# Attention scores of a two-layer decoder trunk: one fp32 product, or three products of high and low parts

## The chip, the cores and the metric

The kernel runs on one core of a Trainium2 chip. The core has five engines that run their own instruction streams and wait for each other by semaphores: TensorE (in the profile PE for the matmuls and PEld for the loads of the stationary operand), VectorE (DVE), ScalarE (ACT), GpSimd (POOL) and SyncE (SP, which here issues the large transfers). Data lies in an on-chip memory of 128 partitions; matmuls write into a second one, PSUM. The metric is the device time of one execution in microseconds, the median of several.

## The reference, cut to what matters

A batch of one sequence of 256 tokens of width 2048 goes through two layers: a Mamba-2 layer, and then a layer of sliding-window attention with 32 query heads of 64, 4 shared key/value heads and a sink per head. Each layer is added to its input, scaled, and normalized. The change touches the scores of the second layer only:

```python
proj = x @ w_in                                   # 2048 -> 2048 q, 2048 gate
q = _rope_partial(proj[..., :Q_WIDTH] + q_bias)    # 32 heads of 64
k, v = _shared_kv(x, kv_w, kv_b, cos, sin)         # 4 heads of 64
s = einsum("bcqhrd,bckhd->bchrqk", q, k) * 64 ** -0.5   # window 128, blocks of 128
s = where(valid, s, -inf)
m = maximum(max(s), sink);  p = exp(s - m)
p = p / (sum(p) + exp(sink - m))
o = (p @ v) * silu(gate)
return o @ w_out
```

## The kernel before, in words

All large matmuls work with split operands. A weight arrives in fp32 (`wr`), ScalarE rounds it to fp32r (`wh`, line 133), VectorE subtracts to get the rest (`wl`, line 134), and three products, high-high, high-low and low-high, are summed in PSUM (lines 195 to 197, 255 to 257, 704 to 706). fp32r is a rounded fp32 that TensorE multiplies in one pass; the profile prints it as f32. Weights come in units of 2048 columns, two units ahead of their use (`next_unit`), through 5 raw, 4 high and 4 low buffers. PSUM has four buffers `mm` for the large products and four buffers `ax` for everything else.

The first layer takes up to about 690 us. Then the normalized stream is held as x1H and x1L, and the second layer runs in blocks of four units, in the order of `B_ORDER`: queries of group j (`q_block`), gates of group j (`gate_block`), output projections ("o"). Group j is one key/value head with its 8 query heads. Smaller steps are put between the units by `later(n, fn)`: fn is called at the n-th `tick` from there, one tick per unit from the query blocks on. A scheduler then orders each engine's instructions and assigns the buffers: tiles of one tag share that tag's `bufs` buffers, and the next tile waits for all readers of the last.

The steps around the scores are these:
- The key/value projection writes `kd` (line 719) and `vt`; each key head is doubled so that it stands on partitions 0 to 63 and 64 to 127 after the transposes of `ktr` (line 731). ScalarE copies them from PSUM to `kT` (line 734).
- `q_block` adds the bias row (line 753, from a row that `bias_row` loads through POOL's queue, line 682), rotates, and one tick later `qtr` transposes (line 759) and ScalarE scales by 0.125 into `qT` (line 763). Two heads stand one above the other on the partitions.
- `attend(j, h)` follows for the half h of the sequence (128 rows): the score products with 64 rows (line 796), the halves of the partitions `par` 0 and 1, against 128 keys (h = 0) or 256 (h = 1); the mask addition from PSUM into `p` (line 801); the maximum (809), the exponentials on ScalarE (815), the division (820). `attend(j, 1)` comes three ticks after `attend(j, 0)`, for j = 3 one tick.
- Three ticks after attend, `turn_p` transposes p through PSUM (lines 829 to 836); later `pv` multiplies with the values (843) and the gate into `o` (849), which is split into oH and oL (858, 859) for the output projection.

The buffers that matter: `p0` and `p1` (one each, for h = 0 and 1), `qt` (two, for kd and the query tiles), `o` (one), `sg` (two, the gates), `bias` (two).

Of the kernel before, what the change touches and what calls it, by code (L numbers as in the profile page):

```python
# [8 lines left out]
F32 = mybir.dt.float32  # L9
F32R = mybir.dt.float32r  # L10
I32 = mybir.dt.int32
AF = mybir.ActivationFunctionType
ALU = mybir.AluOpType
AX = mybir.AxisListType

P = 128
S = 256
# [40 lines left out]
def trunk(ctx: ExitStack, tc: tile.TileContext, A: dict, out: bass.AP, dbg=None):  # L58
    nc = tc.nc
    PSUM = bass.MemoryType.PSUM  # L60

    def pool(name, bufs=1, side=None, space=None, stack=ctx):
        kw = {"space": space} if space is not None else {}
        return stack.enter_context(
            tc.tile_pool(name=name, bufs=bufs, side=side, reuse_waits="tile", **kw)
        )
# [9 lines left out]
    def nm(s):  # L76
        uid[0] += 1
        return f"{s}_{uid[0]}"

    def mm_tile():  # L80
        return mm_ps.tile([P, 512], F32, tag="mm", name=nm("mm"), bufs=4)
# [119 lines left out]
    def later(n, fn):  # L201
        pending.append([n, fn])
# [385 lines left out]
    for g in range(NG):  # L588
        t = 10 * g
# [86 lines left out]
    bp = pool("bp")  # L676
# [1 line left out]
    nc.gpsimd.dma_start(snk, A["snk"].partition_broadcast(P))  # L678

    def bias_row(src):  # L680
        t = bp.tile([P, 512], F32, tag="bias", name=nm("bias"), bufs=2)
        nc.gpsimd.dma_start(t[:], src.partition_broadcast(P))
        return t

# [14 lines left out]
    def x_stat(ps, h, u, ui):  # L699
        for k in range(4):  # L700
            kk = ui * 4 + k
            ks = slice(k * 512, (k + 1) * 512)
            hs = slice(h * P, (h + 1) * P)
            nc.tensor.matmul(ps[:], x1H[:, kk, hs], u.h[:, ks], start=kk == 0, stop=False)  # L704
            nc.tensor.matmul(ps[:], x1L[:, kk, hs], u.h[:, ks], start=False, stop=False)  # L705
            nc.tensor.matmul(ps[:], x1H[:, kk, hs], u.l[:, ks], start=False, stop=kk == KT - 1)  # L706


    kT = bp.tile([P, 4, S], F32, tag="kT", name="kT")
    vt = bp.tile([P, 2, S], F32, tag="vt", name="vt")  # L710
    kvb = bias_row(A["kvb"])
    kv_u = []
    for h in range(2):
        ps = mm_tile()
        for ui in range(4):
            if h == 0:
                kv_u.append(next_unit())
            x_stat(ps, h, kv_u[ui], ui)
        kd = bp.tile([P, 4, 2, 64], F32, tag="qt", name=nm("kd"), bufs=2)
        nc.vector.tensor_tensor(  # L720
            kd[:, :, 0, :], ps[:, :256].rearrange("p (j d) -> p j d", j=4),
            kvb[:, :256].rearrange("p (j d) -> p j d", j=4), ALU.add,
        )
        nc.vector.tensor_tensor(vt[:, h, :], ps[:, 256:], kvb[:, 256:], ALU.add)
        rope(kd[:, :, 0, :], h, 4)
        nc.gpsimd.tensor_copy(kd[:, :, 1, :], kd[:, :, 0, :])

        def ktr(h=h, kd=kd):
            pt = ax_tile()
            for j in range(4):  # L730
                nc.tensor.transpose(
                    pt[:, j * P : (j + 1) * P], kd[:, j, :, :].rearrange("p a d -> p (a d)"), ident
                )
            nc.scalar.copy(kT[:, :, h * P : (h + 1) * P], pt[:].rearrange("p (j t) -> p j t", j=4))

        later(2, ktr)

    qT = {}
    sg = {}
    os_ = {}  # L740

    def q_block(j):
        pss = [mm_tile(), mm_tile()]
        qb = bias_row(A["qb"][j * 512 : (j + 1) * 512])
        for ui in range(4):
            u = next_unit()
            for h in range(2):
                x_stat(pss[h], h, u, ui)
            tick()
        for h in range(2):  # L750
            qt = bp.tile([P, 8, 64], F32, tag="qt", name=nm("qt"), bufs=2)
            qf = qt[:].rearrange("p a d -> p (a d)")
            nc.vector.tensor_tensor(qf, pss[h][:], qb[:], ALU.add)
            rope(qt[:], h, 8)

            def qtr(h=h, qf=qf):
                pt = ax_tile()
                for p_ in range(4):
                    nc.tensor.transpose(
                        pt[:, p_ * P : (p_ + 1) * P], qf[:, p_ * P : (p_ + 1) * P], ident  # L760
                    )
                q2 = bp.tile([P, 4, P], F32, tag="qT", name=nm("qT"), bufs=2)
                nc.scalar.activation(
                    q2[:], pt[:].rearrange("p (a t) -> p a t", a=4), AF.Copy, scale=0.125
                )
                qT[j, h] = q2

            later(1, qtr)

# [14 lines left out]
    def attend(j, h):  # L784

        nk = P * (h + 1)
        q2 = qT[j, h]
        p = bp.tile([P, 8, nk], F32, tag=f"p{h}", name=nm("p"), bufs=1)
        mask = mask_a1 if h else mask_a0
        per = 512 // nk  # L790
        for b in range(0, 4, per):
            pss = [ax_tile(), ax_tile()]
            for i in range(per):
                for par in range(2):
                    rows = slice(64 * par, 64 * par + 64)
                    nc.tensor.matmul(
                        pss[par][:, i * nk : (i + 1) * nk], q2[rows, b + i, :], kT[rows, j, :nk],
                        start=True, stop=True,
                    )
            for par in range(2):  # L800
                nc.vector.tensor_tensor(
                    p[:, par * 4 + b : par * 4 + b + per, :],
                    pss[par][:].rearrange("p (a k) -> p a k", a=per),
                    mask.unsqueeze(1).to_broadcast([P, per, nk]), ALU.add,
                )
        sk = snk[:, j * 8 : j * 8 + 8]
        sm = bp.tile([P, 8, 8], F32, tag="sm", name=nm("sm"), bufs=2)
        mx, ng, rs, es, ri = [sm[:, i, :] for i in range(5)]
        nc.vector.tensor_reduce(mx, p[:], AX.X, ALU.max)
        nc.vector.tensor_tensor(mx, mx, sk, ALU.max)  # L810
        nc.vector.tensor_scalar(ng, mx, -1.0, None, ALU.mult)
        nc.vector.tensor_tensor(es, sk, ng, ALU.add)
        nc.scalar.activation(es, es, AF.Exp)
        for r in range(8):
            nc.scalar.activation(
                p[:, r, :], p[:, r, :], AF.Exp, bias=ng[:, r : r + 1], accum_out=rs[:, r : r + 1]
            )
        nc.vector.tensor_tensor(rs, rs, es, ALU.add)
        nc.vector.reciprocal(ri, rs)
        nc.vector.tensor_tensor(p[:], p[:], ri.unsqueeze(2).to_broadcast([P, 8, nk]), ALU.mult)  # L820

        pts = {}

        def turn_p():
            for kc in range(h + 1):
                for par in range(2):
                    pt = ax_tile()
                    for a in range(4):
                        nc.tensor.transpose(
                            pt[:, a * P : (a + 1) * P], p[:, par * 4 + a, kc * P : (kc + 1) * P], ident  # L830
                        )
                    t = bp.tile([P, 512], F32, tag="pt", name=nm("pt"), bufs=4)
                    if par:
                        nc.scalar.copy(t[:], pt[:])
                    else:
                        nc.vector.tensor_copy(t[:], pt[:])
                    pts[kc, par] = t

        def pv():
            ov = ax_tile()  # L840
            for kc in range(h + 1):
                for par in range(2):
                    nc.tensor.matmul(
                        ov[64 * par : 64 * par + 64, :], vt[:, kc, j * 64 : j * 64 + 64], pts[kc, par][:],
                        start=kc == 0, stop=kc == h,
                    )
            o = bp.tile([P, 4, P], F32, tag="o", name=nm("o"), bufs=1)
            hs = slice(h * P, (h + 1) * P)
            nc.vector.scalar_tensor_tensor(
                o[:], ov[:].rearrange("p (a t) -> p a t", a=4), 0.5, sg[j][:, :, hs], ALU.mult, ALU.mult  # L850
            )
            if j not in os_:
                os_[j] = (
                    bp.tile([P, 4, S], F32R, tag="oH", name=nm("oH"), bufs=2),
                    bp.tile([P, 4, S], F32R, tag="oL", name=nm("oL"), bufs=2),
                )
            oH, oL = os_[j]
            nc.scalar.activation(oH[:, :, hs], o[:], AF.Copy)
            nc.vector.tensor_tensor(oL[:, :, hs], o[:], oH[:, :, hs].bitcast(F32), ALU.subtract)

        last = j == 3
        later(3, turn_p)
        later(4 if last or h else 6, pv)
        if h == 0:
            later(1 if last else 3, lambda: attend(j, 1))
# [153 lines left out]
```

## Time and profile before

| what | value |
|---|---|
| median of the three runs | 1024.12 us |
| the three runs | 1023.79, 1024.12, 1253.01 us |
| the profiled execution's own time | 1023.71 us |
| its span, first to last instruction | 1021.9 us |
| mean granted TensorE clock | 0.997 of full speed |
| read from HBM | 200.13 MB, 198 GB/s over the span |
| score products (line 796): instructions, median duration | 128, 374 ns |
| score products: first and last start | 738.6 us, 954.7 us |

A row of the order of time has the start in us, the length in us, engine, line, operation, tiles (out<-in), rows*columns of the stationary operand, moving operand, and how many instructions are merged into the row; a bracket gives idle time before it and what ended it. A row of the groups has after the count the busy us and the mean ns of one, then the idle time before. A row of waits has the waiter, what it waited for, the total in us, how often, and the longest.

### The profile page before, as it was taken

The numbers are of one execution on the slowest core, as the hardware profiler recorded it, in microseconds if no ns is written. First come the engines' busy times: TensorE is split into PE (matmuls) and PEld (weight loads), VectorE is DVE, ScalarE is ACT, GpSimd is POOL, SyncE is SP. The second block draws the span as 40 slices with busy tenths as digits, with TensorE's granted clock in tenths as the row PEclk, the third lists the DMA queues.
The fourth block names the chain that finished last, engine by engine and source line by source line (L and its number), as shares of the span: only waits on it lengthen the run. The fifth ranks groups of instructions, "written<-read, shape, count | busy, mean of one in ns | idle before, by whom it ended". The sixth has DMA issues, their size and how long they took to land. (4 is left out here: it accounts for less than half of the span.)

```text
span 1021.9 us, 17613 instructions
## 1 busy us (share of the span) xinstructions
PE 1002.5 (98%) x7028; PEld 906.6 (89%) x7028; DVE 806.3 (79%) x1234; ACT 521.7 (51%) x795; POOL 84.9 (8%) x112
## 2 busy tenths in 40 slices
PE   7999999999999999999999999999999999999997
PEld 7998999999998998999999999878988878879975
DVE  6889897886895995986897797798577785785776
ACT  6565554744654554564464474535545453453642
POOL 0000303003003001100300300301000000000002
PEclk9999999999999999999999999999999999999999
DMA  8887585674764765666567466646555445545522
GB/s 307 281 301 241 167 270 176 226 235 141 260 212 143 266 202 192 213 208 219 178 207 239 159 196 229 241 145 234 195 167 170 154 142 182 173 142 182 193 97 82
DMA packets 55730, 203.50 MB, mean 199 GB/s; under 512 B 6288, under 2 KB 6560, under 8 KB 54880
## 3 DMA queue, kind: packets, MB, share of 16 engines
q1 hardware_dynamic: 54288, 196.33, 57.2%
q0 software_dynamic: 1072, 5.53, 1.6%
q8 instruction: 55, 0.90, 0.4%
q10 hardware_dynamic: 288, 0.52, 0.1%
q14 instruction: 27, 0.22, 0.1%
HBM read 200.13 MB, written 2.23 MB: 198 GB/s over the span
## 5 line engine op out<-in xcount | busy, mean ns | idle before, releaser
L134 DVE TENSOR_TENSOR wl<-wr,wh 128x1024 fp32r<-128x1024 f32 (+2 forms) x342 | 393.5, 1169 | 103.0 <-ACT wh L133 101.5
L133 ACT ACTIVATE wh<-wr 128x1024 fp32r<-128x1024 f32 (+2 forms) x342 | 338.0, 1012 | 230.8 <-PE mm L196 67.2
L195 PE MATMUL mm<-xH,wh 128*128 128x256 f32 x1296 | 361.7, 279 | 7.8 <-ACT wh L153 6.0
L197 PE MATMUL mm<-xH,wl 128*128 128x256 f32 x1296 | 360.3, 278 | 3.1 <-DVE wl L134 3.1
L196 PE MATMUL mm<-xL,wh 128*128 128x256 f32 x1296 | 360.7, 279 | 0.0
L195 PEld LDWEIGHTS mm<-xH,wh 128*128 128x128 f32 x1296 | 245.3, 189 | 9.8 <-ACT wh L153 6.3
L197 PEld LDWEIGHTS mm<-xH,wl 128*128 128x128 f32 x1296 | 245.2, 189 | 3.6 <-DVE wl L134 3.5
L196 PEld LDWEIGHTS mm<-xL,wh 128*128 128x128 f32 x1296 | 245.4, 189 | 1.1
L255 PE MATMUL mm<-wh,yH 128*128 128x512 f32 x256 | 101.4, 396 | 0.0
L256 PE MATMUL mm<-wh,yL 128*128 128x512 f32 x256 | 99.9, 390 | 0.0
L257 PE MATMUL mm<-wl,yH 128*128 128x512 f32 x256 | 99.7, 390 | 0.0
L482 POOL TENSOR_TENSOR yz<-yz,z 128x256 f32<-128x256 f32 x32 | 29.8, 931 | 538.5 <-DVE yz L475 538.5
L195 PE MATMUL mm<-x1H,wh 128*128 128x256 f32 x256 | 71.9, 281 | 0.0
L197 PE MATMUL mm<-x1H,wl 128*128 128x256 f32 x256 | 71.0, 277 | 0.0
L196 PE MATMUL mm<-x1L,wh 128*128 128x256 f32 x256 | 71.0, 277 | 0.0
L356 DVE SCALAR_TENSOR_TENSOR cv<-mm,pc,cv 128x255 f32<-128x255 f32 x144 | 68.6, 476 | 2.5 <-ACT cv L354 1.6
L704 PE MATMUL mm<-wh,x1H 128*128 128x512 f32 x160 | 63.3, 396 | 0.0
L706 PE MATMUL mm<-wl,x1H 128*128 128x512 f32 x160 | 62.7, 392 | 0.2 <-DVE wl L134 0.2
L705 PE MATMUL mm<-wh,x1L 128*128 128x512 f32 x160 | 62.7, 392 | 0.2 <-DVE x1L L668 0.2
L255 PEld LDWEIGHTS mm<-wh,yH 128*128 128x128 f32 x256 | 48.1, 188 | 10.3 <-DVE z L421 0.9
L257 PEld LDWEIGHTS mm<-wl,yH 128*128 128x128 f32 x256 | 48.1, 188 | 10.1
L256 PEld LDWEIGHTS mm<-wh,yL 128*128 128x128 f32 x256 | 48.1, 188 | 9.0
(181 smaller groups left out, 1308.5 us busy)
## 6 DMA issues: line engine op xcount, KB each, us to landing
wr<-in_wa SPq DMA_DIRECT2D x158, 512.0 KB, 5.2
wr<-in_wo SPq DMA_DIRECT2D x64, 512.0 KB, 5.3
rb<-rscr SPq DMA_DIRECT2D x32, 512.0 KB, 4.8
wr<-in_wq SPq DMA_DIRECT2D x32, 512.0 KB, 4.5
wr<-in_wg SPq DMA_DIRECT2D x32, 512.0 KB, 5.3
wr<-in_wb SPq DMA_DIRECT2D x32, 512.0 KB, 4.6
wr<-in_wkv SPq DMA_DIRECT2D x8, 512.0 KB, 6.6
first<-in_first SPq DMA_DIRECT2D x4, 512.0 KB, 8.8
```

What stands on the lines that cost most here:

```text
L133: nc.scalar.activation(h[:, sl], raw, AF.Copy)
L134: nc.vector.tensor_tensor(l[:, sl], raw, h[:, sl].bitcast(F32), ALU.subtract)
L195: nc.tensor.matmul(ps, ah, bh, start=first, stop=False)
L196: nc.tensor.matmul(ps, ah, bl, start=False, stop=False)
L197: nc.tensor.matmul(ps, al, bh, start=False, stop=last)
L255: nc.tensor.matmul(ps[:], aH[:, k, hs], u.h[:, ks], start=k == 0, stop=False)
L256: nc.tensor.matmul(ps[:], aL[:, k, hs], u.h[:, ks], start=False, stop=False)
L257: nc.tensor.matmul(ps[:], aH[:, k, hs], u.l[:, ks], start=False, stop=k == 3)
L356: nc.vector.scalar_tensor_tensor(a[:, sft:], ps[:, : S - sft], w(3 - sft), a[:, sft:], ALU.mult, ALU.add)
L704: nc.tensor.matmul(ps[:], x1H[:, kk, hs], u.h[:, ks], start=kk == 0, stop=False)
L705: nc.tensor.matmul(ps[:], x1L[:, kk, hs], u.h[:, ks], start=False, stop=False)
L706: nc.tensor.matmul(ps[:], x1H[:, kk, hs], u.l[:, ks], start=False, stop=kk == KT - 1)
```

## The change

Keys and queries are kept as a high part in fp32r and a low part, the rest in fp32r: `kH`, `kL` in place of `kT`, and `qH`, `qL` in place of `qT`. ScalarE writes the high part from PSUM, VectorE the low part from the same PSUM tile. The score product becomes a sum of three products with 64 rows: qH with kH, qL with kH, qH with kL, the two partition halves alternating. To make room, the bias rows have one buffer, both halves' `p` share one buffer of 8 x 256 (for j = 3, h = 0 `p` takes a buffer of the gates `sg`), and `o` uses the two `qt` buffers.

```diff
@@ -678,7 +678,7 @@
     nc.gpsimd.dma_start(snk, A["snk"].partition_broadcast(P))
 
     def bias_row(src):
-        t = bp.tile([P, 512], F32, tag="bias", name=nm("bias"), bufs=2)
+        t = bp.tile([P, 512], F32, tag="bias", name=nm("bias"), bufs=1)
         nc.gpsimd.dma_start(t[:], src.partition_broadcast(P))
         return t
 
@@ -706,7 +706,8 @@
             nc.tensor.matmul(ps[:], x1H[:, kk, hs], u.l[:, ks], start=False, stop=kk == KT - 1)
 
 
-    kT = bp.tile([P, 4, S], F32, tag="kT", name="kT")
+    kH = bp.tile([P, 4, S], F32R, tag="kH", name="kH")
+    kL = bp.tile([P, 4, S], F32R, tag="kL", name="kL")
     vt = bp.tile([P, 2, S], F32, tag="vt", name="vt")
     kvb = bias_row(A["kvb"])
     kv_u = []
@@ -731,7 +732,10 @@
                 nc.tensor.transpose(
                     pt[:, j * P : (j + 1) * P], kd[:, j, :, :].rearrange("p a d -> p (a d)"), ident
                 )
-            nc.scalar.copy(kT[:, :, h * P : (h + 1) * P], pt[:].rearrange("p (j t) -> p j t", j=4))
+            hs = slice(h * P, (h + 1) * P)
+            v = pt[:].rearrange("p (j t) -> p j t", j=4)
+            nc.scalar.activation(kH[:, :, hs], v, AF.Copy)
+            nc.vector.tensor_tensor(kL[:, :, hs], v, kH[:, :, hs].bitcast(F32), ALU.subtract)
 
         later(2, ktr)
 
@@ -759,11 +763,13 @@
                     nc.tensor.transpose(
                         pt[:, p_ * P : (p_ + 1) * P], qf[:, p_ * P : (p_ + 1) * P], ident
                     )
-                q2 = bp.tile([P, 4, P], F32, tag="qT", name=nm("qT"), bufs=2)
-                nc.scalar.activation(
-                    q2[:], pt[:].rearrange("p (a t) -> p a t", a=4), AF.Copy, scale=0.125
+                qH, qL = [bp.tile([P, 4, P], F32R, tag=t, name=nm(t), bufs=2) for t in ("qH", "qL")]
+                v = pt[:].rearrange("p (a t) -> p a t", a=4)
+                nc.scalar.activation(qH[:], v, AF.Copy, scale=0.125)
+                nc.vector.scalar_tensor_tensor(
+                    qL[:], v, 0.125, qH[:].bitcast(F32), ALU.mult, ALU.subtract
                 )
-                qT[j, h] = q2
+                qT[j, h] = qH, qL
 
             later(1, qtr)
 
@@ -784,19 +790,24 @@
     def attend(j, h):
 
         nk = P * (h + 1)
-        q2 = qT[j, h]
-        p = bp.tile([P, 8, nk], F32, tag=f"p{h}", name=nm("p"), bufs=1)
+        qH, qL = qT[j, h]
+        if j == 3 and h == 0:
+
+            p = bp.tile([P, 8, nk], F32, tag="sg", name=nm("p"), bufs=2)
+        else:
+            p = bp.tile([P, 8, S], F32, tag="p", name=nm("p"), bufs=1)[:, :, :nk]
         mask = mask_a1 if h else mask_a0
         per = 512 // nk
         for b in range(0, 4, per):
             pss = [ax_tile(), ax_tile()]
             for i in range(per):
-                for par in range(2):
-                    rows = slice(64 * par, 64 * par + 64)
-                    nc.tensor.matmul(
-                        pss[par][:, i * nk : (i + 1) * nk], q2[rows, b + i, :], kT[rows, j, :nk],
-                        start=True, stop=True,
-                    )
+                for n, (q2, k2) in enumerate(((qH, kH), (qL, kH), (qH, kL))):
+                    for par in range(2):
+                        rows = slice(64 * par, 64 * par + 64)
+                        nc.tensor.matmul(
+                            pss[par][:, i * nk : (i + 1) * nk], q2[rows, b + i, :], k2[rows, j, :nk],
+                            start=n == 0, stop=n == 2,
+                        )
             for par in range(2):
                 nc.vector.tensor_tensor(
                     p[:, par * 4 + b : par * 4 + b + per, :],
@@ -844,7 +855,7 @@
                         ov[64 * par : 64 * par + 64, :], vt[:, kc, j * 64 : j * 64 + 64], pts[kc, par][:],
                         start=kc == 0, stop=kc == h,
                     )
-            o = bp.tile([P, 4, P], F32, tag="o", name=nm("o"), bufs=1)
+            o = bp.tile([P, 4, P], F32, tag="qt", name=nm("o"), bufs=2)
             hs = slice(h * P, (h + 1) * P)
             nc.vector.scalar_tensor_tensor(
                 o[:], ov[:].rearrange("p (a t) -> p a t", a=4), 0.5, sg[j][:, :, hs], ALU.mult, ALU.mult
```

## The prediction

> **What bounds the kernel now.** I read the head of the page first, then the busy time by stretches over the attention part (from about 690 us), then who TensorE waited for there, and last the order of time around the scores.
>
> ```profile
> span 1021.9 us, 17613 instructions
> PE 1002.5 (98%) x7028; PEld 906.6 (89%) x7028; DVE 806.3 (79%) x1234; ACT 521.7 (51%) x795; POOL 84.9 (8%) x112
> ```
> ```profile
> 714.00:976.00 262.00, 260.89 (x1649) 223.40 (x1648) 186.03 (x291) 133.00 (x278) 2.14 (x4) 1.00 0.52 172
> ```
> ```profile
> PE ax L829 <- DVE o L849: 1.0, 1, 1.0
> PE mm L705 <- DVE x1L L668: 0.2, 1, 0.2
> ```
>
> The columns of the second fence are the stretch, its length, then busy us of PE, PEld, DVE, ACT and POOL, the granted clock and the DMA share. All score products lie in this stretch, PE has work in 260.9 of 262 us at full clock, and the third fence (waiter, releaser, us in total, times, longest) says that from 690 to 1010 us it waited 1.2 us in all. So a change here costs what it adds to PE's own instruction stream, plus any wait it creates. A matmul's duration is no price, since matmuls overlap; the price is the step from one start to the next.
>
> ```profile
> 740.51 0.28 PE L195 MATMUL mm<-x1H,wh 128*128 128x256 f32 x1
> ...
> 744.93 0.28 PE L195 MATMUL mm<-x1H,wh 128*128 128x256 f32 x1
> ```
> ```profile
> L195 PE MATMUL mm<-xH,wh 128*128 128x256 f32 x1296 | 361.7, 279 | 7.8 <-ACT wh L153 6.0 <-DVE cv L356 1.8
> L731 PE MATMUL ax<-cc,kd 128*128 128x128 f32 x8 | 1.0, 272 | 0.0
> ```
> ```profile
> 714.76 1.03 PE L731 MATMUL ax<-cc,kd 128*128 128x128 f32 x8
> ```
> ```profile
> 119.00 0.52 PEld L506 LDWEIGHTS ax<-cc,sq 128*128 128x128 f32 x4
> ```
>
> Between the two rows of the first fence lie 39 matmuls of 256 columns in the rounded fp32 type (fp32r, which the profile prints as f32): 4.42 / 39 = 0.113 us a step, in one pass. The weight load has a step of its own: four loads whose matmuls stream a single column each take (0.52 - 0.19) / 3 = 0.11 us, and eight transposes of 128 columns step at (1.03 - 0.27) / 7 = 0.109. So a matmul with few moving columns doesn't go below about 0.11 us here: I read this as the load binding it.
>
> **The scores as they are.** The order of time shows three of the eight bursts (PE, and PEld for the loads); a row merges what stands together, and its second column is the length.
>
> ```profile
> 738.61 1.16 PE L796 MATMUL ax<-kT,qT 64*128 64x128 f32 x16
> 739.70 0.39 PE L195 MATMUL mm<-x1H,wh 128*128 128x256 f32 x1
> ```
> ```profile
> 738.61 0.97 PEld L796 LDWEIGHTS ax<-kT,qT 64*128 64x128 f32 x16
> ```
> ```profile
> 953.11 2.00 PE L796 MATMUL ax<-kT,qT 64*128 64x256 f32 x16
> 955.03 0.39 PE L195 MATMUL mm<-x1H,wh 128*128 128x256 f32 x1
> ```
> ```profile
> 953.10 1.60 PEld L796 LDWEIGHTS ax<-kT,qT 64*128 64x128 f32 x16
> ```
> ```profile
> 757.17 1.16 PEld L796 LDWEIGHTS ax<-kT,qT 64*128 64x128 f32 x10 [0.17 <-PE ax L829]
> 758.83 0.73 PEld L796 LDWEIGHTS ax<-kT,qT 64*128 64x128 f32 x6 [0.51 <-ACT pt L834]
> 759.89 0.19 PEld L704 LDWEIGHTS mm<-wh,x1H 128*128 128x128 f32 x1 [0.33 <-issue]
> ```
> ```profile
> PEld ax L796 <- ACT pt L834: 1.3, 3, 0.5
> ```
>
> The code asks for 8 products per call of attend; the trace has 16. So an fp32 product is two instructions, and the two 64-row halves (`par`) go side by side: 16 instructions are 8 pairs. For the first half of the sequence (h = 0, 128 keys) the loads give (0.97 - 0.19) / 7 = 0.111 us a pair; for h = 1 (256 keys) the first step is a bare load of 0.11 and the rest (1.60 - 0.19 - 0.11) / 6 = 0.217. That is about twice the 256-column step of 0.113, so each instruction streams its columns twice, and one fp32 product streams them four times. A burst costs its pairs and about 0.20 us at its ends: 8 x 0.111 + 0.20 = 1.09 (739.70 - 738.61), 8 x 0.217 + 0.19 = 1.92 (955.03 - 953.11). For j = 0 to 2 (the last fence counts three) the h = 1 burst has a wait in its middle: the second group of two heads starts at 758.83, when ACT has emptied the transposes' buffer, and takes 1.06 us to 759.89.
>
> **The change part by part.**
>
> Scores, L796. Each product becomes three fp32r products of one pass, in the order high-high, low-high, high-low, halves alternating: 12 pairs for 8, and the loads grow from 8 to 12 with them. With 256 keys I take 0.113 a pair, the row of the same size and type. For j = 3: 12 x 0.113 - 8 x 0.217 = 1.36 - 1.74 = -0.38 us. For j = 0 to 2 the first group ends earlier, but the second still starts when the buffer is free, so only that group gains: 6 x 0.113 - 4 x 0.217 = -0.19, three times -0.57. With 128 keys no row has fp32r at 128 columns. The bounds: half the 256-column step, 0.056, if loads were free, and 0.217, four passes as in plain fp32. I take 0.111, since the load step of 0.11 stands both in the single-column row and in the scores' own loads. Then 12 x 0.111 - 8 x 0.111 = +0.44 for a burst, four of them +1.78. By that the change buys passes where 256 columns stream and loses where the load rules. Sum on PE: 1.78 - 0.38 - 0.57 = +0.83 us. The ends of a burst stay (8 bursts before and after).
>
> Low parts on DVE. New: kL twice and qL eight times, each a 128x512 subtraction out of PSUM into fp32r, as L668 does it. High parts on ACT: the same instructions as now with another output type.
>
> ```profile
> L668 DVE TENSOR_TENSOR x1L<-ax,x1H 128x512 fp32r<-128x512 f32 x8 | 5.4, 686 | 0.2
> L667 ACT ACTIVATE x1H<-ax 128x512 fp32r<-128x512 f32 x8 | 4.8, 597 | 6.5 <-PE ax L662 6.4
> L734 ACT COPY kT<-ax 128x512 f32<-128x512 f32 x2 | 1.1, 578 | 0.0
> ```
> ```profile
> L763 ACT ACTIVATE qT<-ax x8: 581/588/599, 733.0 to 941.3; 128x512 f32<-128x512 f32 x8
> ```
>
> 10 x 0.686 = 6.9 us more DVE work; ACT 2 x 0.019 + 8 x 0.009 = 0.1 us. I cost both at nothing. What hides them is the lead of the weight splits, DVE's main duty (L134), over their use:
>
> ```profile
> 827.60 2.36 DVE L134 TENSOR_TENSOR wl<-wr,wh 128x1024 fp32r<-128x1024 f32 x2
> ```
> ```profile
> 841.80 0.40 PE L706 MATMUL mm<-wl,x1H 128*128 128x512 f32 x1
> ```
>
> This is the shortest lead of the weight units read after 717 us, where the first low parts come (one more is like it): the first half of the unit is done at about 828.8 and read at 841.8, 13 us later. One qL pair puts 1.4 us in front of it. If the cover were gone, 6.9 us would be added. The scores now also need qL: qT was written at 733.0 for scores at 738.6, and qL follows qH by one DVE instruction and what stands in DVE's line, some 2 us; 3 us stay.
>
> Bias rows, two buffers to one. The load of the first query bias is no longer issued ahead but after the last reader of the key/value bias; later ones wait for the query block before.
>
> ```profile
> 706.03 0.54 POOL L682 DMA_DIRECT2D bias<-in_qb  x1 [0.70 <-DVE vt L724]
> ```
> ```profile
> L753 DVE TENSOR_TENSOR qt<-mm,bias x8: 680/686/692, 724.4 to 934.5; 128x512 f32<-128x512 f32 x8
> ...
> DMA to landing us min/median/max: 3.6/4.8/5.9
> ```
>
> The key/value bias is free at the time of this row, 706.0; the first reader of the query bias is at 724.4; landing takes at most 5.9, so 12 us are left. Behind it on POOL stands only the second copy of the keys, and the issue occupies 0.54 us. Cost nothing; with the cover gone, up to 5.9 us once.
>
> Buffer p. One buffer of 8x256 for both halves. The next writer is attend(j, 1), whose mask additions now wait for the transposes of p of (j, 0) (L829); in the trace these stand on PE just ahead of the (j, 1) scores (757.17 waits for them). For (3, 0) p goes into a gate buffer whose reader finished one block before. Cost nothing; were the transposes late, mask additions, not PE, would be late first.
>
> Buffer o joins the two `qt` buffers. There is one place where they collide: o of (0, 0) is written while the second query block's two tiles fill the pair.
>
> ```profile
> 777.34 0.68 DVE L753 TENSOR_TENSOR qt<-mm,bias 128x512 f32<-128x512 f32 x1
> 777.94 0.68 DVE L849 SCALAR_TENSOR_TENSOR o<-ax,sg 128x512 f32<-128x512 f32 x1
> ```
> ```profile
> 786.70 1.09 PE L759 MATMUL ax<-cc,qt 128*128 128x128 f32 x8
> ```
>
> Either qt or o has to wait. If o waits for the transposes of qt, it comes at 787.8 instead of 777.9, DVE's line may stand up to 9.9 us, and one of four PSUM buffers stays taken. The 13 us lead covers 9.9; I cost it at nothing, and at 9.9 without cover.
>
> The sum: 0.83 us. The profiled execution took 1023.71 us (span 1021.9 and 1.8 around it), 0.41 below the median of 1024.12. That gives 1024.54 against the one and 1024.95 against the other; I put 1024.7.
>
> **The rivals.**
>
> Four passes at 128 columns. Against it: nothing measured, since all fp32r matmuls here have 256 or 512 columns; that is also all that speaks for it. Price: 12 x (0.217 - 0.111) x 4 = +5.1, 1029.8.
>
> The halves don't go side by side in fp32r. Against it: fp32 halves do, and the new order alternates them. Price: 12 x 0.111 x 4 = 5.3 for h = 0, 12 x 0.113 = 1.36 for j = 3, 6 x 0.113 x 3 = 2.0 for the second groups: +8.7, 1033.4.
>
> [...]
>
> The change doesn't do what it says, and this is the slower one: with 64 rows each of the three products costs a whole fp32 product, two instructions of two passes. 24 steps for 12: 12 x 0.111 x 4 = 5.3; j = 3: 24 x 0.217 - 1.36 = 3.8; for j = 0 to 2 the second groups 12 x 0.217 - 0.68 = 1.9 each, and the first groups outgrow their wait by 12 x 0.217 + 0.1 - 1.66 = 1.0 each, 8.8 in all. Together +17.9, 1042.6. It decides for slower by 2% (1044.6) once the 256-column step is 0.24 us or more in place of 0.217. Against it: the 1296 fp32r matmuls at line 195 run in one pass, though with 128 rows.
>
> The collision of o and qt with its cover gone: +9.9, 1034.6.
>
> ```profile
> L796 PE MATMUL ax<-kT,qT 64*128 64x256 f32 x64 | 10.1, 399 | 0.1
> ...
> L796 PE MATMUL ax<-kT,qT 64*128 64x128 f32 x64 | 4.6, 285 | 0.0
> ```
>
> **How the numbers follow.** Load-bound forecast 0.60, with a range of its own from 1022.9 (without the 1.8 lost at 128 keys) to 1026.5 (without the 0.95 gained at 256 keys, and 0.9 for small waits); four passes 0.17; load hidden 0.09; halves in turn 0.06; whole fp32 products 0.04; collision 0.04. The range 1021.8 to 1030.6 holds the first three, 0.86: 0.3 below the hidden load, 0.8 above the four passes. A measurement of this kernel tells about 2% from no change. Faster by that needs -20.5 us, and the scores' matmuls are 10.1 + 4.6 us busy in all (the rows above): 0.01. Slower by that: the upper half of the whole-product case and a rest for a wait that I don't see, 0.03. Within 2%: 0.96.
>
> **What the profile after would show.** The score line at 24 products a burst with 24 loads, in pairs; h = 0 bursts of about 1.5 us and the j = 3, h = 1 burst of about 1.55, against 1.09 and 1.92; the second groups at 0.88 instead of 1.06. DVE about 7 us busier, PE's waits between 690 and 1010 us still near 1.2 us. The forecast is wrong if the 128-key step is 0.06 or 0.2, if the loads of the two halves don't start together, or if PE waits for qL, o or a weight split.

## The result, and the profile after

| | before | after |
|---|---|---|
| median | 1023.87 us (20 runs) | 1027.24 us (20 runs) |
| ratio to before, 95% interval | 1 | 1.0028 [1.0019, 1.0037] |
| profiled execution: own time, span | 1023.71, 1021.9 us | 1027.93, 1026.2 us |
| mean granted TensorE clock | 0.997 | 0.994 |

The changed kernel is 2.9 us slower by the ratio (0.0028 x 1024; interval 1.9 to 3.8; the medians differ by 3.4): far inside 2%, and inside the predicted range, but the forecast was +0.8 and the interval doesn't hold that. The ratio leaves out one run of before that took 1253.01 us. So the question is where the other 2 us came from. The head of the page after comes first, then the order of time of PE around the first score burst (128 keys) and the last one (256 keys).

```profile
span 1026.2 us, 17755 instructions
PE 1003.4 (98%) x7092; PEld 909.2 (89%) x7092; DVE 812.4 (79%) x1244; ACT 520.4 (51%) x795; POOL 84.8 (8%) x112
```
```profile
738.81 0.33 PE L807 MATMUL ax<-kH,qH 64*128 64x128 f32 x2
738.97 0.28 PE L807 MATMUL ax<-kH,qL 64*128 64x128 f32 x2
...
740.09 0.28 PE L807 MATMUL ax<-kL,qH 64*128 64x128 f32 x2
740.30 0.38 PE L195 MATMUL mm<-x1H,wh 128*128 128x256 f32 x1
```
```profile
954.39 0.39 PE L807 MATMUL ax<-kH,qH 64*128 64x256 f32 x2
...
955.81 0.28 PE L807 MATMUL ax<-kL,qH 64*128 64x256 f32 x2
956.02 0.38 PE L195 MATMUL mm<-x1H,wh 128*128 128x256 f32 x1
```

DVE is 6.1 us busier (812.4 - 806.3): the ten low parts. Each row of the second fence is a pair (x2): the two halves of the partitions still go side by side. From the second pair to the twelfth are ten steps in 1.12 us, 0.112 us a step at 128 keys. The burst takes 740.30 - 738.81 = 1.49 us (before 1.09), and the one of j = 3, h = 1 takes 956.02 - 954.39 = 1.63 (before 1.92). These are close to the forecast's 1.5 and 1.55. So the scores did nearly what was predicted, and the rest lies elsewhere. Next are the waits of PE from 690 to 1015 us, and the place of the longest one in the order of time, after and before.

```profile
PE ax L840 <- DVE o L860: 2.6, 1, 2.6
PE ax L807 <- ACT pt L845: 1.5, 3, 0.6
```
```profile
973.49 1.08 PE L854 MATMUL ax<-pt,vt 128*64 128x512 f32 x4
974.50 1.53 PE L840 MATMUL ax<-cc,p 128*128 128x128 f32 x12
...
976.33 0.40 PE L257 MATMUL mm<-wl,oH 128*128 128x512 f32 x1
979.30 0.66 PE L840 MATMUL ax<-cc,p 128*128 128x128 f32 x4 [2.57 <-DVE o L860]
...
980.04 0.63 PE L256 MATMUL mm<-wh,oL 128*128 128x512 f32 x1
...
983.43 0.40 PE L255 MATMUL mm<-wh,oH 128*128 128x512 f32 x1
...
986.26 1.94 PE L854 MATMUL ax<-pt,vt 128*64 128x512 f32 x8
```
```profile
972.49 1.08 PE L843 MATMUL ax<-pt,vt 128*64 128x512 f32 x4
973.50 1.53 PE L829 MATMUL ax<-cc,p 128*128 128x128 f32 x12
976.00 0.66 PE L829 MATMUL ax<-cc,p 128*128 128x128 f32 x4 [0.97 <-DVE o L849]
...
982.04 1.94 PE L843 MATMUL ax<-pt,vt 128*64 128x512 f32 x8
```

The row of 1.5 us is not new: before, it stood as the load queue's wait of 1.3 us for the same buffer. The first row is the finding. In the last group the values product of (3, 0) (L854) fills an `ax` buffer, VectorE empties it into `o` (L860), and the last four transposes of p of (3, 1) wait for that buffer. This wait stood in the profile before with 1.0 us, and the prediction quoted it. It is now 2.6.

Behind it in the changed kernel, eight matmuls of 512 columns step at (983.43 - 980.04) / 8 = 0.42 us; the steps before and after that are 0.23. The busy time by stretches shows the granted clock there (the column ahead of the DMA share):

```profile
976.60:980.00 3.40, 0.83 (x6) 0.69 (x6) 3.40 (x6) 1.02 (x3) 0.00 (x0) 1.00 0.80 258
980.00:983.40 3.40, 3.40 (x9) 2.64 (x8) 2.17 (x3) 0.86 (x2) 0.00 (x0) 0.50 0.81 260
983.40:986.80 3.40, 3.40 (x17) 2.32 (x17) 2.25 (x3) 0.66 (x1) 0.00 (x0) 1.00 0.25 92
```

For 3.4 us the clock is at half speed. From the first score product to the last values product, the stretch that holds all the change's steps, it was 982.04 - 738.61 = 243.43 us before and is 986.26 - 738.81 = 247.45 now: +4.02. Of that the scores are 0.8, the longer wait 1.60, and the half-speed steps 8 x (0.42 - 0.23) = 1.5.

Why does `o` come later? VectorE's order of time in front of it, before and after:

```profile
969.14 0.17 DVE L818 TENSOR_TENSOR sm<-sm 128x8 f32<-128x8 f32 x1 [0.89 <-ACT p L815]
...
969.58 2.29 DVE L820 TENSOR_TENSOR p<-p,sm 128x2048 f32<-128x2048 f32 x1
971.79 0.68 DVE L264 TENSOR_TENSOR xr<-xr,mm 128x512 f32<-128x512 f32 x1
972.39 2.35 DVE L134 TENSOR_TENSOR wl<-wr,wh 128x1024 fp32r<-128x1024 f32 x2
974.66 0.68 DVE L264 TENSOR_TENSOR xr<-xr,mm 128x512 f32<-128x512 f32 x1
975.26 0.68 DVE L849 SCALAR_TENSOR_TENSOR o<-ax,sg 128x512 f32<-128x512 f32 x1
```
```profile
970.41 0.17 DVE L829 TENSOR_TENSOR sm<-sm 128x8 f32<-128x8 f32 x1 [2.05 <-ACT p L826]
...
971.20 0.64 DVE L847 COPY pt<-ax 128x512 f32<-128x512 f32 x1
971.76 2.28 DVE L831 TENSOR_TENSOR p<-p,sm 128x2048 f32<-128x2048 f32 x1
973.96 1.22 DVE L134 TENSOR_TENSOR wl<-wr,wh 128x1024 fp32r<-128x1024 f32 x1
975.09 0.68 DVE L264 TENSOR_TENSOR xr<-xr,mm 128x512 f32<-128x512 f32 x1
975.69 1.22 DVE L134 TENSOR_TENSOR wl<-wr,wh 128x1024 fp32r<-128x1024 f32 x1
976.83 0.68 DVE L264 TENSOR_TENSOR xr<-xr,mm 128x512 f32<-128x512 f32 x1
977.42 1.22 DVE L134 TENSOR_TENSOR wl<-wr,wh 128x1024 fp32r<-128x1024 f32 x1
978.56 0.68 DVE L860 SCALAR_TENSOR_TENSOR o<-ax,sg 128x512 f32<-128x512 f32 x1
```

None of the change's own VectorE instructions stands here. The scheduler has put three halves of weight splits (L134) between the division of p and `o`, where there were two. From the start of the division to the start of `o` it is 6.80 us, before 5.68, which is 1.12 more. The division itself also comes later against PE's work: the values product starts 1.73 us after the division's start (973.49 - 971.76), before 2.91, which is 1.18 less. Of these 1.18 us, 0.9 are order too. VectorE stood idle in front of the division until ScalarE had the exponentials (2.05 us, before 0.89), and an accumulation (L264) and a copy of transposes (L847, before L836), which came ahead of that idle time before, now stand behind it. So `o` comes 2.30 us later against PE's work; three matmuls of the output projection, which PE now runs ahead of the last transposes, cover 0.7 of it, and 1.6 are left. PE doesn't wait for work that was added; it waits for work that was put into another order.

### The profile page after: what moved, and what is told of

Its sections match the earlier page's. It is cut to its first block, busy times and chain, and to the rows that moved or that the text cites. A ratio compares the mean times of both kernels' runs of the same rounds, so it can differ in the third digit from the quotient of the medians.

```text
span 1026.2 us, 17755 instructions
## 1 busy us (share of the span) xinstructions
PE 1003.4 (98%) x7092; PEld 909.2 (89%) x7092; DVE 812.4 (79%) x1244; ACT 520.4 (51%) x795; POOL 84.8 (8%) x112
## 5 line engine op out<-in xcount | busy, mean ns | idle before, releaser
L134 DVE TENSOR_TENSOR wl<-wr,wh 128x1024 fp32r<-128x1024 f32 (+2 forms) x342 | 393.2, 1168 | 99.0 <-ACT wh L133 97.2
```

Source lines behind the costliest of these rows:

```text
L134: nc.vector.tensor_tensor(l[:, sl], raw, h[:, sl].bitcast(F32), ALU.subtract)
```

## The experiments

Each was run beside the kernel before, on the same chip. The column "stretch" is the profiled time from the first score product to the last values product, worked out from the order of time as above, against 243.43 us.

| kernel | PE's wait for `o` | stretch, against before | ratio to before, 95% |
|---|---|---|---|
| before with the buffer changes | 1.0 us | +0.03 us | 0.9999 [0.9989, 1.0009] |
| after with one fp32 product | 1.0 | -0.05 | 1.0007 [0.9996, 1.0018] |
| after, values of (3, 0) in an `mm` buffer | none | -0.35 | 0.9996 [0.9983, 1.0009] |
| after, three products only for h = 1 | 0.5 | -1.22 | 0.9993 [0.9984, 1.0003] |
| before, `o` of (3, 0) written three times | 1.1, for a copy | +0.14 | 1.0000 [0.9988, 1.0012] |
| after with filler matmuls in the wait | 0.5 | +3.22 | 1.0036 [1.0022, 1.0050] |
| before, values of (3, 0) in an `mm` buffer | none | -1.18 | 0.9991 [0.9976, 1.0006] |
| h = 1 alone, and the `mm` buffer | none | -1.84 | 0.9984 [0.9971, 0.9997] |
| after, once more | 2.6 | +2.53 | 1.0037 [1.0023, 1.0051] |
| after, h = 0 streams 256 keys | 0.3 | +0.74 | 1.0009 [0.9995, 1.0024] |

**Is it the buffers?** Only the buffer edits of the change, in the kernel before:

```diff
-        t = bp.tile([P, 512], F32, tag="bias", name=nm("bias"), bufs=2)
+        t = bp.tile([P, 512], F32, tag="bias", name=nm("bias"), bufs=1)
...
-        p = bp.tile([P, 8, nk], F32, tag=f"p{h}", name=nm("p"), bufs=1)
+        if j == 3 and h == 0:
+            p = bp.tile([P, 8, nk], F32, tag="sg", name=nm("p"), bufs=2)
+        else:
+            p = bp.tile([P, 8, S], F32, tag="p", name=nm("p"), bufs=1)[:, :, :nk]
...
-            o = bp.tile([P, 4, P], F32, tag="o", name=nm("o"), bufs=1)
+            o = bp.tile([P, 4, P], F32, tag="qt", name=nm("o"), bufs=2)
```

> The kernel before with only the buffer changes (one bias row, p shared, o in the query tiles' pair); scores stay one fp32 product. Order theory (the three products shift VectorE's order in the last group, o of (3, 0) leaves PSUM later, PE stands 2.7 us instead of 1.1 and then falls to half clock for 3.4 us): nothing of this comes from the buffers, so 0 within 0.5 us of before, wait of the transposes for o near 1.0 us. Buffer theory (o or p waits for its shared buffer): +2 to +3 us and the wait near 2.6 us. Vector theory (ten more subtractions push VectorE back): 0.

Measured: 1023.17 us, ratio 0.9999 [0.9989, 1.0009], the wait for `o` at 1.0 us. The buffers cost nothing, the collision of `o` and `qt` included.

**Is it VectorE's extra work?** The changed kernel with one fp32 product of the high parts; the two products with the low parts are left out, while the low parts are still written.

```diff
-                for n, (q2, k2) in enumerate(((qH, kH), (qL, kH), (qH, kL))):
-                    for par in range(2):
-                        rows = slice(64 * par, 64 * par + 64)
-                        nc.tensor.matmul(
-                            pss[par][:, i * nk : (i + 1) * nk], q2[rows, b + i, :], k2[rows, j, :nk],
-                            start=n == 0, stop=n == 2,
-                        )
+                for par in range(2):
+                    rows = slice(64 * par, 64 * par + 64)
+                    nc.tensor.matmul(
+                        pss[par][:, i * nk : (i + 1) * nk],
+                        qH[rows, b + i, :].bitcast(F32), kH[rows, j, :nk].bitcast(F32),
+                        start=True, stop=True,
+                    )
```

> The changed kernel with the low parts written as there but not used: one fp32 product of the high parts, so the low-part products are left out. Buffers and VectorE's extra work stay, the two extra products go. Order theory: score bursts back at 1.09 and 1.92 us, wait for o near 1.0 us, 0 within 0.5 us of before. Vector theory: VectorE has its ten instructions more, so wait for o near 2.6 us and +2 to +3 us. Buffer theory: +2 to +3 us as well.

Measured: 1024.58 us, ratio 1.0007 [0.9996, 1.0018]. PE's wait in the same place is the old one:

```profile
PE ax L840 <- DVE o L860: 1.0, 1, 1.0
```

Ten more instructions on VectorE and the new buffers together leave the wait at 1.0 us. So the longer wait comes in with the three products on PE, although it is VectorE that is late.

**Does the rest of the loss hang on that wait?** The changed kernel, with the values product of (3, 0) in an `mm` buffer, so that the transposes have a free `ax` buffer:

```diff
-            ov = ax_tile()
+            ov = mm_tile() if j == 3 and h == 0 else ax_tile()
```

> The changed kernel with the values' product of (3, 0) in a PSUM buffer of the large products, so that the transposes of (3, 1) have all four small buffers and need not wait for o; VectorE's order in that group stays the changed one. Order theory: the 2.7 us stand of PE and the half clock behind it go, the score steps (+0.8 us) stay, before's own 1.1 us stand is saved: between -0.8 and +0.5 us of before. Vector or buffer theory: the late chain stays late, PE stands elsewhere in that group, +2 to +3 us remain. A price that could show: a wait for a large buffer, up to 1 us.

Measured: 1023.76 us, ratio 0.9996 [0.9983, 1.0009]. PE's order of time there:

```profile
972.75 1.08 PE L854 MATMUL mm<-pt,vt 128*64 128x512 f32 x4
973.76 1.97 PE L840 MATMUL ax<-cc,p 128*128 128x128 f32 x16
```

All 16 transposes stand in one row, with no wait, and the granted clock behind them is 1.00 up to 990 us. The three products are all still there, VectorE's order is still the new one (three halves of a split, `o` at 977.83), and the kernel is level with before. The same edit in the kernel before says what its own 1.0 us was worth:

> The kernel before with the values' product of (3, 0) in a large PSUM buffer. Scores and VectorE's order untouched. The 1.1 us stand of PE goes: -1.1 us of before. If a wait for a large buffer takes its place: 0.

Measured: the stretch is 1.18 us shorter; the median, 1022.56 us, ratio 0.9991 [0.9976, 1.0006], doesn't resolve it. The two kernels with this edit differ by -0.35 + 1.18 = 0.83 us in the stretch: the price of the scores alone.

**Are 128 keys the losing half?** The changed kernel with three products for h = 1 and the old fp32 product for h = 0, first with the wait, then with the `mm` buffer as well. The cut leaves out that the keys of the first half are copied in fp32 too, and that its queries are kept in fp32 in place of the two parts:

```diff
-                for n, (q2, k2) in enumerate(((qH, kH), (qL, kH), (qH, kL))):
+                terms = ((qH, kH), (qL, kH), (qH, kL)) if h else ((qH, kT),)
+                for n, (q2, k2) in enumerate(terms):
...
```

> The changed kernel with the three products only for 256 keys; for 128 keys plain fp32 keys and queries are kept as before (their low parts not written for queries of the first half). VectorE's order in the last group is then that of before. Order theory: first-half bursts 1.09 us, second-half j = 3 burst 1.63, wait for o near 1.0 us, no half clock there: -0.7 us of before. Vector theory: six of ten instructions stay, +1 to +2 us. Buffer theory: +2 to +3 us. If the load step did not bind at 128 columns, nothing would be won by going back to fp32 there.

> Three products for 256 keys only, and the values' product of (3, 0) in a large PSUM buffer: the two gains together, 0.75 us of scores and the stand of 1.1 us, so -1.9 us of before, and faster than the run with the three products for 256 keys alone. If the stand is covered anyway: -0.7 us.

Measured: 1022.70 us, 0.9993 [0.9984, 1.0003], and 1022.72 us, 0.9984 [0.9971, 0.9997]. The bursts at 128 keys are back at 1.09 us, those at 256 keys keep their gain; the stretches are 1.22 and 1.84 us below before. The first gained more than was expected, since its wait is 0.5 us and not 1.0. The second kernel has the shortest stretch of the study and is the only one whose interval lies below 1; it beats before by 1.6 us (0.3 to 3.0). That it is faster than the first doesn't show in the medians, only in the stretches.

**Can the wait be made in the kernel before?** `o` of (3, 0) was written three times, so that PE would stand longer with the old scores:

```diff
-            nc.vector.scalar_tensor_tensor(
-                o[:], ov[:].rearrange("p (a t) -> p a t", a=4), 0.5, sg[j][:, :, hs], ALU.mult, ALU.mult
-            )
+            for _ in range(3 if j == 3 and h == 0 else 1):
+                nc.vector.scalar_tensor_tensor(
+                    o[:], ov[:].rearrange("p (a t) -> p a t", a=4), 0.5, sg[j][:, :, hs], ALU.mult, ALU.mult
+                )
```

> The kernel before with one thing doubled: VectorE writes o of (3, 0) three times instead of once, the same value, so that PSUM is let go some 2.4 us later. The scores are untouched. Order theory: PE's stand before the last transposes grows from 1.1 to about 2.8 us, which costs 1.7 us, and a half-clock stretch of 3.4 us follows it and costs about 1.6 more: +3 us together, like the changed kernel without its products. If the half clock has another cause than the stand: +1.7 us and full clock. If the stand is covered by something: 0.

Measured: 1023.62 us, ratio 1.0000 [0.9988, 1.0012]. The expectation missed, because the edit didn't make the wait:

```profile
978.84 0.66 PE L829 MATMUL ax<-cc,p 128*128 128x128 f32 x4 [1.09 <-DVE pt L836]
```

The transposes now took another buffer and waited 1.09 us for a copy (L836). The scheduler had answered the edit, so this run tests nothing of the wait's price. It shows how easily one more instruction turns the order.

**Does the half-speed stretch belong to the wait?** Twelve matmuls of 512 columns on finished data, read by nobody, were put into the wait; then the changed kernel was run once more.

```diff
+                    if j == 3 and h == 1 and kc == 1 and par == 1:
+                        d, z = mm_tile(), os_[2][0]
+                        for _ in range(12):
+                            nc.tensor.matmul(
+                                d[:], z[:, 0, :P], z[:, 0:2, :].rearrange("p a s -> p (a s)"),
+                                start=True, stop=True,
+                            )
```

> The changed kernel with 12 matmuls of 512 columns, whose result nobody reads, put on PE where it stands (between the third and the fourth transposed block of (3, 1)). They take about 2.7 us, so nothing is waited for less, only PE is busy meanwhile; three matmuls of the output block that now run there come behind, up to 0.7 us more. Half-clock theory: the clock stays full behind the stand, so about -1 us against the changed kernel (+2 us of before instead of +3). If the half clock is not tied to PE standing idle: +3 to +4 us of before and a half-clock stretch near 980 us.

> The changed kernel itself a second time, to see whether the half-speed stretch behind TensorE's stand recurs. Theory A (scores +0.8, a stand 1.6 us longer, and behind it a half-speed stretch that belongs to the stand): the wait for o is again 2.6 us, the matmuls behind it again take about 0.63 instead of 0.40 us for some 3 us, and the median is 1027 us, ratio 1.003. Theory B (the half-speed stretch is chance and only sometimes there): the wait is again 2.6 us, the matmuls behind it take 0.40 us, and the profiled execution is 1 to 1.6 us shorter than the first one, about 1026.5 us.

Measured with the filler: 1027.91 us, ratio 1.0036 [1.0022, 1.0050]. The half-speed stretch is gone (granted clock 1.00 from 976 to 990 us), but the median isn't lower, so the gain of about 1 us that was expected missed. The second profile of the changed kernel tells why. It has the same wait, and no half speed behind it (granted clock 1.00 from 960 to 1020 us):

```profile
739.94 0.33 PE L807 MATMUL ax<-kH,qH 64*128 64x128 f32 x2
```
```profile
980.51 0.66 PE L840 MATMUL ax<-cc,p 128*128 128x128 f32 x4 [2.58 <-DVE o L860]
...
981.24 0.39 PE L256 MATMUL mm<-wh,oL 128*128 128x512 f32 x1
981.47 0.40 PE L257 MATMUL mm<-wl,oH 128*128 128x512 f32 x1
...
985.90 1.94 PE L854 MATMUL ax<-pt,vt 128*64 128x512 f32 x8
```

Its stretch is 985.90 - 739.94 = 245.96 us, +2.53 against before, of which 0.8 are the scores and 1.61 the wait. Its median is 1027.33 us, ratio 1.0037 [1.0023, 1.0051]. So Theory B of that expectation holds: the half speed came in one of the two profiles, and the loss is there without it. Theory B's own time, 1026.5 us for the profiled execution, was missed (1027.58): this execution lost 1.1 us in the first layer, with its first score product at 739.94 instead of 738.81; half speed (the granted clock in slices of 0.1 us) lasted 6.8 us there (81.0 to 87.8), in the first profile 3.4 (82.3 to 85.7). And the filler kernel's stretch of 246.65 us is the second profile's plus three useful matmuls that the filler pushed out of the wait, 3 x 0.23 = 0.7 us.

**Can more work on PE make it faster?** The changed kernel, where the scores for h = 0 stream all 256 keys; the upper 128 columns aren't read.

```diff
-        per = 512 // nk
+        per = 2
...
-                            pss[par][:, i * nk : (i + 1) * nk], q2[rows, b + i, :], k2[rows, j, :nk],
+                            pss[par][:, i * S : (i + 1) * S], q2[rows, b + i, :], k2[rows, j, :],
...
-                    pss[par][:].rearrange("p (a k) -> p a k", a=per),
+                    pss[par][:].rearrange("p (a k) -> p a k", a=per)[:, :, :nk],
```

> The changed kernel, where the scores of the first half of the sequence stream all 256 keys instead of 128 (the upper 128 columns are computed and not read; twice the PSUM groups of two heads). Theory A (the load of the 64-row halves sets the step at 128 columns): the columns are nearly free, the step goes from 0.107 to the 0.113 us of 256 columns, a burst without a wait from 1.49 to about 1.56 us, four of them +0.3 us (a wait for a free PSUM buffer in the middle, as in the second half's bursts, would come on top). Rival (the columns set the step): 12 pairs at twice 0.107 give 2.8 us a burst, +5.2 us in all.

The order of time of its first burst on PE, and of VectorE in front of `o`:

```profile
740.58 0.28 PE L807 MATMUL ax<-kH,qL 64*128 64x256 f32 x2
...
741.76 0.28 PE L807 MATMUL ax<-kL,qH 64*128 64x256 f32 x2
```
```profile
972.04 2.29 DVE L831 TENSOR_TENSOR p<-p,sm 128x2048 f32<-128x2048 f32 x1
974.25 0.68 DVE L264 TENSOR_TENSOR xr<-xr,mm 128x512 f32<-128x512 f32 x1
974.84 2.36 DVE L134 TENSOR_TENSOR wl<-wr,wh 128x1024 fp32r<-128x1024 f32 x2
977.12 0.68 DVE L264 TENSOR_TENSOR xr<-xr,mm 128x512 f32<-128x512 f32 x1
977.71 0.68 DVE L860 SCALAR_TENSOR_TENSOR o<-ax,sg 128x512 f32<-128x512 f32 x1
```

Twice the columns cost 0.118 us a step (1.18 / 10) in place of 0.112, as the load-bound theory expects and far from the rival's doubling; a burst takes 1.62 us. The surprise is the total: 1024.86 us, ratio 1.0009 [0.9995, 1.0024], where the changed kernel beside it took 1027.33. With more work on PE it is faster, because VectorE's order is the old one again, with two halves of a split in front of `o`, and PE's wait there is 0.3 us. Neither theory had that in its expectation. All work of the change is there, and more, and the long wait is gone with the new order: the change's work alone doesn't make it. The edit also doubles the mask additions for h = 0, so it doesn't tell which property the scheduler's order answered to.

## Why the prediction was right or wrong

- **Scores on PE: right.** Forecast +1.78 for the four h = 0 bursts, measured 4 x (1.49 - 1.09) = 1.6. Forecast -0.38 for j = 3, h = 1, measured 1.63 - 1.92 = -0.30. Forecast -0.57 for the second groups; the three bursts shrank from 2.72, 2.63 and 2.63 us to 2.57, 2.49 and 2.47, by 0.45 in all, always from their first row to the next row behind them. The sum is 0.85 against 0.83, but that it fits so well is in part luck: at 128 keys 0.2 less was lost than forecast, at 256 keys, where a step took 0.118 us and not 0.113, 0.2 less was gained.
- **The load binds at 128 keys: right.** Step 0.112 (taken: 0.111), and twice the columns add 0.006. The rivals of four passes, halves in turn, whole fp32 products and a hidden load all fall. No run shows the hidden load, which had 0.09 of the chances and set the lower end of the range: it needed a step below the 0.111 us of the scores' own loads, and the step was 0.112.
- **Low parts, bias rows, p and `o` buffers cost nothing: right**, by the first two experiments (1.0 us of wait, ratios of 0.9999 and 1.0007).
- **"PE's waits between 690 and 1010 us still near 1.2 us": wrong**, and this is the step that failed. The wait for `o` went from 1.0 to 2.6 us. The prediction had quoted this very row, named a wait for o as a sign of being wrong, and still took the row as a fixed sum. It was a race between PE and VectorE that the kernel before already lost by 1 us, in the last group, where the weight splits stand between the division of p and `o` and VectorE has no gap from the one to the other. There the lead of 13 us that covered everything else didn't apply: it belongs to the splits' readers, not to `o`.
- **What the forecast didn't ask: what the scheduler does.** It took every instruction to stay in its place. The scheduler gave VectorE a new order, and 1.6 us of the 2.5 us that the second profile lost came from that. No term of the sum stood for it; the likeliest case's own range ended at 1026.5 with 0.9 us "for small waits", and the median was 0.7 above it. That the whole range held the median is luck: its upper part was there for four passes at 128 columns (1029.8), which the step of 0.112 us rules out.

With 0.8 for the scores and 1.6 for the wait the sum is +2.4, and both intervals of the changed kernel, 1.9 to 3.8 and 2.4 to 5.2 us, hold it, or end there. How often the half-speed stretch comes on top (1.5 us, in one profile of two) stays open, and so does what exactly in the three products turned the scheduler's order; that its own estimate of their length did it was not tried by itself.

## What to carry to other kernels

A wait that the profile before shows on the bounding engine, however short, is a race already lost: ask what stands in front of the late instruction and what a new order there would cost, since what it grows by goes to the end (here 1.6 of the 2.5 us). Where a scheduler orders the engines, compare the orders of both kernels around such places before believing a sum of durations; a run that undoes the wait alone (here one buffer) separates the work's price from the order's. And the split product gained at 256 keys (1.92 to 1.63 us a burst) and lost at 128 (1.09 to 1.49), so it pays to choose per size.

## What the runs showed of the hardware

After the same wait of 2.6 us, the clock fell to half speed for 3.4 us in one profile of the changed kernel (0.50 in 980.00 to 983.40, quoted above) and not in the other, where the wait ends at 980.51:

```profile
976.00:980.00 4.00, 1.93 (x15) 1.45 (x13) 4.00 (x6) 2.11 (x2) 0.00 (x0) 1.00 0.50 141
980.00:984.00 4.00, 3.49 (x18) 2.94 (x18) 4.00 (x7) 1.59 (x3) 0.00 (x0) 1.00 0.78 241
984.00:990.00 6.00, 6.00 (x27) 3.62 (x26) 4.93 (x6) 2.64 (x3) 0.00 (x0) 1.00 0.27 98
```

The 3.4 us up to the wait's end hold the same work on PE in both: 3.40 - 2.57 = 0.83 us in the first profile, 3.40 - 2.58 = 0.82 in the second. So neither the length of the wait nor PE's work in that time tells the two apart, and what decides whether such a wait costs 1.5 us more is not shown.

A product in fp32r is one instruction in these traces, at 0.113 us a step with 256 columns; one in fp32 is two, at 0.217 us each, 1.9 times as long: one pass and four passes are read from that.

The runs also show that the two 64-row halves go side by side in fp32r as they do in fp32, at 0.112 us a pair with 128 columns and 0.118 with 256.
